# Two-layer decoder trunk: which FFN chunks go through the seven-product down projection

## The chip, the cores and the metric

The kernel runs on one core of a Trainium2 chip. The metric is the device time of one execution in microseconds, as the median of several executions; three of the kernel before gave 998.08, 990.7 and 993.01 us. The engines are TensorE (PE, with its weight loads shown apart as PEld), VectorE (DVE), ScalarE (ACT), GpSimd (POOL) and SyncE (SP), whose queue here issues the weight transfers.

## The reference

Two layers, each made of a half-step FFN, a token mixing and a second half-step FFN, on one sequence of 256 tokens with 1024 channels in float32. An FFN has 2816 hidden channels. What matters here is this:

```python
def swiglu(x, w_gate, w_up, w_down):
    return (jax.nn.silu(x @ w_gate) * (x @ w_up)) @ w_down
...
for l in range(DEPTH):
    x = layer_norm(ALPHA * x + 0.5 * swiglu(x, ffn1_gate[l], ...), ln1_g[l], ln1_b[l])
    proj = x @ w_in[l]            # short convolution, spatial gating, sparse attention
    ...
    mix = jnp.concatenate([y_a, y_b, y_c], axis=-1) @ w_out[l]
    x = layer_norm(ALPHA * x + mix, ln2_g[l], ln2_b[l])
    x = layer_norm(ALPHA * x + 0.5 * swiglu(x, ffn2_gate[l], ...), ln3_g[l], ln3_b[l])
```

## The kernel before

**Products.** Every large matrix product is done as three TensorE matmuls in a reduced float32 format: an operand is split into a high part (`hi`) and the rest (`lo`), and hi·hi, hi·lo and lo·hi are summed in PSUM. `mm3` (L248 to L250) does this for 512 output columns and `proj_chan` (L258 to L260) for the chunks whose output lies with channels on partitions, 256 tokens wide. `split_to` (L263) makes the two parts: ACT casts the high part, DVE subtracts it from the source.

**Weights.** All weights come in one order, made by `_plan()` (L72 on). `ensure` (L166 on) issues the next tile's transfer on SP into a `raw` buffer (5 of them), has ACT cast it (L190) and DVE subtract (L191), and puts the result into pools `hi` and `lo` (12 buffers each). It is called by `blocks` with a look-ahead of 7 tiles, so a tile's transfer and casts are written into the program some tiles ahead of its use.

**An FFN.** The hidden channels are cut into chunk 0 of 512 and chunks 1 to 9 of 256. Per chunk, `chan` or `tok` computes gate (`pg`) and up (`pu`), ACT makes `sg` = silu(pg) (L421), DVE makes `h` = pu·sg (L426), and h is split into `hTh` and `hTl` for the down projection. Chunk 0 is computed with tokens on partitions, so its h is transposed on PE (`trans`, L439) before it can be split. Each 128 rows of down weights are one tile `d` of 128x1024.

**Paired chunks.** In the FFNs for which `_paired` is 6 (three of the four; 0 for the first FFN of the program), the down projection of chunks 0 to 5 works on two `d` tiles at a time: the 2x2 blocks of tokens and output columns are multiplied with seven products `M1` to `M7` instead of eight (the Strassen and Winograd scheme). `pair_operands` prepares the weights' side: four DVE subtractions of 128x512 in the raw buffers (L202), one split of 512 columns (`b`), one of 1024, and, in `rest()`, two more splits of 1024 columns (the sums `th` and `sh`); `ensure` puts `rest()` off until a tile or so later. `left_sums` (L461 to L464) makes the left side's four sums `S` of 128x128, split by one more `split_to`. `combine` adds the seven results into x at the end.

**Banks.** While pairs run, `pg` and `pu` share one PSUM bank ("free"), the other holds M3, the "tr" pair holds M6 and M7, and the four "y" banks M1, M2, M4 and M5. So `pu` of a chunk can start only once ACT has read `pg` (`sg`), and the next `pg` only once DVE has read `pu` (`h`). Between the two stand the products of the chunk before: M1, M2, M4 and M5 (12 matmuls) between `pg` and `pu`, M6, M7 and M3 (9 matmuls) after `pu`.

**Order.** Each engine works through its own list, which a scheduler makes from the program, by priorities that the code raises at a few places (`tc.high_priority`). After the mixing, the output projection (`yo`) of tokens 0 to 127 is followed by the layer norm of that half (L374 to L380) and `to_xT` (L280), which transposes x and splits it into `xTh` and `xTl`, while PE does `yo` of the second half; the last attention heads' softmax (`P`, L833) and their transposes (`trp`, L837) fall into the same stretch.

## Time and profile before

| | before |
|---|---|
| median of three executions | 993.01 us (990.7 to 998.08) |
| profiled execution | 994.34 us |
| its span in the trace | 992.6 us |
| PE busy (matmuls) | 969.1 us (98%) |
| PE weight loads busy | 875.8 us (88%) |
| DVE busy | 734.8 us (74%) |
| ACT busy | 512.3 us (52%) |
| DMA | 55%, 183 GB/s over the span |
| granted TensorE clock | 0.999 of full speed |

The busy times are shares of the span. Matmuls are pipelined: a row's length is longer than the time from its start to the next one's start, so a run of matmuls is read by the distance between starts. A row's bracket gives the idle time of its engine ahead of it and what ended that.

### The profile page before, as it was taken

How to read it: one execution, taken by the hardware profiler on the slowest of the kernel's cores; microseconds unless marked ns; L12 is line 12 of the kernel's file. 1: busy time of each engine (PE TensorE's matmuls, PEld its weight loads, DVE VectorE, ACT ScalarE, POOL GpSimd, SP SyncE). 2: the span in 40 equal slices, each digit the busy share in tenths (PEclk: the TensorE clock that was granted, in tenths of full speed). 3: DMA queues.
4: the chain of work that ended last, by engine and by line, in shares of the span. 5: the costliest groups of instructions: out<-in, count | busy, mean ns of one | idle time of the engine just before them, and what ended most of it. 6: DMA issues, size and time to landing. Idle time of an engine off the chain costs nothing.

```text
span 992.6 us, 16879 instructions
## 1 busy us (share of the span) xinstructions
PE 969.1 (98%) x6765; PEld 875.8 (88%) x6765; DVE 734.8 (74%) x1094; ACT 512.3 (52%) x730; POOL 19.8 (2%) x42
## 2 busy tenths in 40 slices
PE   7999999999999999999999999999999999999996
PEld 5899999899878799999879899998988778989995
DVE  5755454586869978877598888848678797888844
ACT  6644444256556655555255556534475555556520
POOL 1000000010000000000000000000000000000000
PEclk9999999999999999999999999999999999999999
DMA  7977566284323557677245667764742245757611
GB/s 256 344 237 226 181 194 193 96 324 147 111 86 128 179 180 236 194 253 233 86 151 171 233 214 253 237 200 148 256 149 80 84 158 170 253 196 232 213 60 43
DMA packets 53069, 183.19 MB, mean 185 GB/s; under 512 B 6656, under 2 KB 7168, under 8 KB 52992
## 3 DMA queue, kind: packets, MB, share of 16 engines
q1 hardware_dynamic: 52992, 182.12, 55.0%
q8 instruction: 53, 0.87, 0.4%
q14 instruction: 24, 0.20, 0.1%
HBM read 181.05 MB, written 1.05 MB: 183 GB/s over the span
## 4 chain that ended last, share of the span: by engine, by line
PE 74%; DVE 11%; DMA 9%; issue 3%; ACT 3%; SPq 0%; DVEq 0%; ACTq 0%
DMA raw<-in_ws 8%; PE pu L258 6%; PE pu L260 6%; PE pu L259 6%; PE pg L258 5%; PE pg L260 5%; PE pg L259 5%; PE y L248 4%; PE y L250 4%; PE y L249 4%; DVE raw L202 3%; PE pc L258 3%; PE pc L260 3%; PE pc L259 3%; DVE lo L263 3%
## 5 line engine op out<-in xcount | busy, mean ns | idle before, releaser
L191 DVE TENSOR_TENSOR lo<-raw,hi 128x1024 fp32r<-128x1024 f32 (+3 forms) x284 | 336.6, 1200 | 115.2 <-ACT hi L190 113.5
L190 ACT CAST hi<-raw 128x1024 fp32r<-128x1024 f32 (+3 forms) x284 | 289.8, 1034 | 247.4 <-PE pu L259 64.7
L258 PE MATMUL pu<-xTh,hi 128*128 128x256 f32 x576 | 161.7, 281 | 3.4 <-ACT sg L421 3.4
L258 PE MATMUL pg<-xTh,hi 128*128 128x256 f32 x576 | 161.6, 281 | 0.5 <-DVE h L426 0.5
L260 PE MATMUL pu<-xTh,lo 128*128 128x256 f32 x576 | 160.9, 279 | 0.0
L260 PE MATMUL pg<-xTh,lo 128*128 128x256 f32 x576 | 160.8, 279 | 0.0
L259 PE MATMUL pu<-xTl,hi 128*128 128x256 f32 x576 | 160.8, 279 | 0.0
L259 PE MATMUL pg<-xTl,hi 128*128 128x256 f32 x576 | 160.8, 279 | 0.0
L258 PEld LDWEIGHTS pu<-xTh,hi 128*128 128x128 f32 x576 | 108.0, 188 | 7.1 <-ACT sg L421 5.9
L263 ACT CAST hi<-raw 128x1024 fp32r<-128x1024 f32 x63 | 66.2, 1052 | 90.5 <-DVE raw L202 46.5
L258 PEld LDWEIGHTS pg<-xTh,hi 128*128 128x128 f32 x576 | 108.1, 188 | 2.3 <-DVE h L426 1.2
L259 PEld LDWEIGHTS pu<-xTl,hi 128*128 128x128 f32 x576 | 107.9, 187 | 1.2
L260 PEld LDWEIGHTS pu<-xTh,lo 128*128 128x128 f32 x576 | 108.2, 188 | 0.2
L259 PEld LDWEIGHTS pg<-xTl,hi 128*128 128x128 f32 x576 | 107.9, 187 | 0.5
L260 PEld LDWEIGHTS pg<-xTh,lo 128*128 128x128 f32 x576 | 108.2, 188 | 0.0
L263 DVE TENSOR_TENSOR lo<-raw,hi 128x1024 fp32r<-128x1024 f32 x63 | 76.7, 1219 | 30.6 <-ACT hi L263 21.7
L258 PE MATMUL pc<-xTh,hi 128*128 128x256 f32 x256 | 73.0, 285 | 0.5 <-DVE kd L630 0.5
L248 PE MATMUL y<-hi,hTh 128*128 128x512 f32 x184 | 72.4, 394 | 0.0
L260 PE MATMUL pc<-xTh,lo 128*128 128x256 f32 x256 | 72.4, 283 | 0.0
L259 PE MATMUL pc<-xTl,hi 128*128 128x256 f32 x256 | 71.8, 281 | 0.0
L250 PE MATMUL y<-hi,hTl 128*128 128x512 f32 x184 | 71.8, 390 | 0.0
L249 PE MATMUL y<-lo,hTh 128*128 128x512 f32 x184 | 71.6, 389 | 0.0
(188 smaller groups left out, 1702.0 us busy)
## 6 DMA issues: line engine op xcount, KB each, us to landing
raw<-in_ws SPq DMA_DIRECT2D x312, 512.0 KB, 4.6
w<-in_ws SPq DMA_DIRECT2D x8, 512.0 KB, 6.2
lng<-in_ln SPq DMA_DIRECT2D x6, 512.0 KB, 6.8
lnb<-in_ln SPq DMA_DIRECT2D x6, 512.0 KB, 7.7
raw<-in_ws SPq DMA_DIRECT2D x8, 256.0 KB, 4.8
raw<-in_ws SPq DMA_DIRECT2D x4, 420.0 KB, 4.3
x<-in_x SPq DMA_DIRECT2D x4, 256.0 KB, 5.6
out<-x SPq DMA_DIRECT2D x4, 256.0 KB, 2.1
```

The costliest lines, as they stand in the source:

```text
L190: splits.append((ACT.copy(hi, raw), DVE.tensor_tensor(lo, raw, hi.bitcast(F32), ALU.subtract)))
L191: DVE.tensor_tensor(lo, raw, hi.bitcast(F32), ALU.subtract)))
L202: sub = lambda o, i, j: DVE.tensor_tensor(o, i, j, ALU.subtract)
L248: PE.matmul(o, lhsT=a[0], rhs=b[0], start=start, stop=False)
L249: PE.matmul(o, lhsT=a[0], rhs=b[1], start=False, stop=False)
L250: return PE.matmul(o, lhsT=a[1], rhs=b[0], start=False, stop=stop)
L258: PE.matmul(p[:, b, :], lhsT=hi, rhs=xTh[:, k, :], start=k == 0, stop=False)
L259: PE.matmul(p[:, b, :], lhsT=hi, rhs=xTl[:, k, :], start=False, stop=False)
L260: PE.matmul(p[:, b, :], lhsT=lo, rhs=xTh[:, k, :], start=False, stop=k == KC - 1)
L263: return ACT.copy(hi, src), DVE.tensor_tensor(lo, src, hi.bitcast(F32), ALU.subtract)
```

## The change

All four FFNs now have seven paired chunks, and these are chunks 1 to 7 in place of 0 to 5. Chunk 0's down weights are taken out of their place in the plan and put just ahead of chunk 9's; its down projection is done plainly at the end of the FFN, with chunks 8 and 9. With chunk 0 out of the pairs, no copy of its transposed h is needed (`hf` goes). The groups of products become M1, M2, M3, M5 and M6, M7, M4. `rest()` is put off one tile further. The raw pool grows from 5 to 7 buffers, `hi` and `lo` shrink from 12 to 11 each, and the work tag "a" grows from 9 to 12.

```diff
--- before.py
+++ after.py
@@ -32,9 +32,12 @@
 
 
 
+RAW, SPLIT = 7, 11
+
+
 def _paired(l, f):
 
-    return 0 if (l, f) == (0, 1) else 6
+    return 7
 
 
 def _w_in_groups():
@@ -83,7 +86,9 @@
                 for name in ("g", "u"):
                     step = _step(l, f, name, c)
                     out += [((l, f, name, c), k, step * fw, True) for k in range(0, KC, step)]
-                out += [((l, f, "d", c), k, 1024, True) for k in range(fw // 128)]
+
+                for c in ([0, c] if c == len(CHUNKS) - 1 else [c] if c else []) if _paired(l, f) else [c]:
+                    out += [((l, f, "d", c), k, 1024, True) for k in range(CHUNKS[c][1] // 128)]
     return out
 
 
@@ -137,9 +142,9 @@
     with ExitStack() as es:
         pool = lambda name, bufs, **k: es.enter_context(tc.tile_pool(name=name, bufs=bufs, **k))
         cst = pool("cst", 1)
-        rawp = pool("raw", 5)
-        hip = pool("hi", 12)
-        lop = pool("lo", 12)
+        rawp = pool("raw", RAW)
+        hip = pool("hi", SPLIT)
+        lop = pool("lo", SPLIT)
         wk = pool("wk", 9)
         sm = pool("sm", 3)
         lnp = pool("lnp", 1)
@@ -168,7 +173,7 @@
             while len(loaded) <= min(i, len(plan) - 1):
                 key, k, n, split, o = plan[len(loaded)]
                 src = A["ws"][o:o + 128 * n].rearrange("(p c) -> p c", p=128)
-                if len(key) == 4 and key[2] == "d" and key[3] < _paired(*key[:2]):
+                if len(key) == 4 and key[2] == "d" and 0 < key[3] <= _paired(*key[:2]):
                     raw = rawp.tile([128, n], F32, name="raw", tag="raw")
                     stream.append(SP.dma_start(raw, src))
                     if k % 2 == 0:
@@ -190,7 +195,7 @@
                 splits.append((ACT.copy(hi, raw),
                                DVE.tensor_tensor(lo, raw, hi.bitcast(F32), ALU.subtract)))
                 loaded.append((hi, lo))
-                while put_off and put_off[0][0] < len(loaded) - 1:
+                while put_off and put_off[0][0] < len(loaded) - 2:
                     put_off.pop(0)[1]()
 
         def pair_operands(ra, rb):
@@ -408,7 +413,7 @@
             def chan(name, c):
 
                 w = kslices((l, f, name, c), 256)
-                if c <= paired_chunks:
+                if 1 < c <= paired_chunks + 1:
                     p = ps.tile([128, 2, 256], F32, name="p" + name, tag=free, bufs=1)
                 else:
                     p = gu_bank([128, 2, 256], "p" + name)
@@ -429,8 +434,8 @@
             hT = {}
 
             def hpair():
-                return (wk.tile([128, 512], F32R, name="hTh", tag="a"),
-                        wk.tile([128, 512], F32R, name="hTl", tag="a"))
+                return (wk.tile([128, 512], F32R, name="hTh", tag="a", bufs=12),
+                        wk.tile([128, 512], F32R, name="hTl", tag="a", bufs=12))
 
             def trans(h, t):
                 tr = ps.tile([128, 512], F32, name="tr", tag="tr")
@@ -438,10 +443,6 @@
                     c = slice(i * 128, i * 128 + 128)
                     PE.transpose(tr[:, c], h[:, c], ident)
                 hT[0, t] = hpair()
-                if paired_chunks:
-                    hf[t] = wk.tile([128, 4, 128], F32, name="hf", tag="w")
-                    ACT.copy(hf[t].rearrange("p a b -> p (a b)"), tr)
-                    tr = hf[t].rearrange("p a b -> p (a b)")
                 split_to(*hT[0, t], tr)
 
             def stationary(c, t, i):
@@ -451,38 +452,31 @@
                 s = slice(i * 256 + t * 128, i * 256 + t * 128 + 128)
                 return hT[c][0][:, s], hT[c][1][:, s]
 
-            hf = {}
             left = {}
             M = {}
 
-            def left_sums(c, i, a11, a12, a21, a22):
-
+            def left_sums(c, h):
+
+                A = {(t, b): h[:, b * 256 + t * 128:b * 256 + t * 128 + 128] for t in range(2) for b in range(2)}
                 S = wk.tile([128, 4, 128], F32, name="S", tag="w")
-                DVE.tensor_tensor(S[:, 0, :], a21, a22, ALU.add)
-                DVE.tensor_tensor(S[:, 1, :], S[:, 0, :], a11, ALU.subtract)
-                DVE.tensor_tensor(S[:, 2, :], a11, a21, ALU.subtract)
-                DVE.tensor_tensor(S[:, 3, :], a12, S[:, 1, :], ALU.subtract)
+                DVE.tensor_tensor(S[:, 0, :], A[1, 0], A[1, 1], ALU.add)
+                DVE.tensor_tensor(S[:, 1, :], S[:, 0, :], A[0, 0], ALU.subtract)
+                DVE.tensor_tensor(S[:, 2, :], A[0, 0], A[1, 0], ALU.subtract)
+                DVE.tensor_tensor(S[:, 3, :], A[0, 1], S[:, 1, :], ALU.subtract)
                 hi, lo = hpair()
                 split_to(hi, lo, S.rearrange("p a b -> p (a b)"))
                 part = lambda j: (hi[:, j * 128:j * 128 + 128], lo[:, j * 128:j * 128 + 128])
-                left[c, i] = {5: part(0), 6: part(1), 7: part(2), 3: part(3)}
-
-            def left_side(c, i, m):
-                if m in (3, 5, 6, 7):
-                    return left[c, i][m]
-                t, b = {1: (0, 0), 2: (0, 1), 4: (1, 1)}[m]
-                return stationary(c, t, 2 * i + b)
+                left[c] = {5: part(0), 6: part(1), 7: part(2), 3: part(3),
+                           1: stationary(c, 0, 0), 2: stationary(c, 0, 1), 4: stationary(c, 1, 1)}
 
             def paired(c, ms):
 
+                w = blocks((l, f, "d", c))[0]
                 for m in ms:
                     if m not in M:
                         tag, bufs = {3: (held, 1), 6: ("tr", 2), 7: ("tr", 2)}.get(m, ("y", 4))
                         M[m] = ps.tile([128, 512], F32, name=f"M{m}", tag=tag, bufs=bufs)
-                    for i in range(CHUNKS[c][1] // 256):
-                        w = blocks((l, f, "d", c))[2 * i]
-                        mm3(M[m], left_side(c, i, m), w[m], c == 0 and i == 0,
-                            c == paired_chunks - 1 and i == CHUNKS[c][1] // 256 - 1)
+                    mm3(M[m], left[c][m], w[m], c == 1, c == paired_chunks)
 
             def combine():
 
@@ -535,22 +529,19 @@
                     if t == 1:
                         trans(h[0], 0)
                     h[t] = product(tok("u", t), sg)
-
-            if paired_chunks:
-                turns.append(1)
-                free, held = f"gu{len(turns) % 2}", f"gu{1 - len(turns) % 2}"
             for c in range(1, n):
+                in_pairs = 1 < c <= paired_chunks + 1
+                if in_pairs and c == 2:
+
+                    turns.append(1)
+                    free, held = f"gu{len(turns) % 2}", f"gu{1 - len(turns) % 2}"
                 p = chan("g", c)
                 with tc.high_priority(offset=60):
                     sg = gated(p)
                 if c == 1:
                     trans(h[1], 1)
-                if c <= paired_chunks:
-                    if c == 1:
-                        for i in range(2):
-                            a = lambda t, b: hf[t][:, 2 * i + b, :]
-                            left_sums(0, i, a(0, 0), a(0, 1), a(1, 0), a(1, 1))
-                    paired(c - 1, (1, 2, 4, 5))
+                if in_pairs:
+                    paired(c - 1, (1, 2, 3, 5))
                 elif not paired_chunks:
                     if c > 1 and c - 2 < n - late:
                         down([c - 2], 1)
@@ -559,14 +550,13 @@
                 pu = chan("u", c)
                 with tc.high_priority(offset=60):
                     hc = product(pu, sg)
-                if c <= paired_chunks:
-                    paired(c - 1, (6, 7, 3))
+                if in_pairs:
+                    paired(c - 1, (6, 7, 4))
                 hT[c] = hpair()
                 split_to(*hT[c], hc)
-                if c < paired_chunks:
-                    a = lambda t, b: hc[:, b * 256 + t * 128:b * 256 + t * 128 + 128]
-                    left_sums(c, 0, a(0, 0), a(0, 1), a(1, 0), a(1, 1))
-                if c == paired_chunks:
+                if c <= paired_chunks:
+                    left_sums(c, hc)
+                if paired_chunks and c == paired_chunks + 1:
                     combine()
                 if c == 2:
                     with tc.issue_after(stream[-1].ins):
@@ -575,9 +565,10 @@
                     with tc.issue_after(stream[-1].ins):
                         mid()
 
-            down(range(n - late, n - 1), 0)
+            cs = [*range(paired_chunks + 1, n - 1), 0] if paired_chunks else [*range(n - late, n - 1)]
+            down(cs, 0)
             down([n - 1], 0, end=True)
-            done = down(range(n - late, n), 1, end=True)
+            done = down([*cs, n - 1], 1, end=True)
             coef = 1.0 if paired_chunks else 2 * ALPHA
             layer_norm(0, y[0], coef, 4 * EPS, gb, last, [done[9], done[14]])
             layer_norm(1, y[1], coef, 4 * EPS, gb, last)
...
```

(The last three places give `kd`, `P` and `PT` the same `bufs=12`.)

What that moves shows at three places. The first is DVE at the start of the second FFN of layer 0, after the mixing, up to the first `h`. L202 is a subtraction of a pair's raw weights, L191 and L263 with `lo` are splits of plain and of pair weights. Before:

```order
L202 TENSOR_TENSOR raw<-raw 128x512
L263 TENSOR_TENSOR xTl<-tr,xTh 128x4x128 x2
L202 TENSOR_TENSOR raw<-raw 128x512
L263 TENSOR_TENSOR lo<-raw,hi 128x1024
L202 TENSOR_TENSOR raw<-raw 128x512 x2
L191 TENSOR_TENSOR lo<-raw,hi 128x1024
L202 TENSOR_TENSOR raw<-raw 128x512
L263 TENSOR_TENSOR lo<-raw,hi 128x1024
L202 TENSOR_TENSOR raw<-raw 128x512
L263 TENSOR_TENSOR lo<-raw,hi 128x1024
L202 TENSOR_TENSOR raw<-raw 128x512
L426 TENSOR_TENSOR h<-pu,sg 128x512
```

The same place after the change (L196 is the split of a plain tile, L431 is `h`):

```order
L384 SCALAR_TENSOR_TENSOR x_80<-x_80,mv,lng 128x512 x2
L385 SCALAR_TENSOR_TENSOR x_80<-x_80,rs,lnb 128x512 x2
L196 TENSOR_TENSOR lo<-raw,hi 128x1024
L268 TENSOR_TENSOR xTl<-tr,xTh 128x4x128 x2
L431 TENSOR_TENSOR h<-pu,sg 128x512
L196 TENSOR_TENSOR lo<-raw,hi 128x1024
L268 TENSOR_TENSOR b_3624<-raw,b_3624 128x512
L207 TENSOR_TENSOR raw<-raw 128x512 x2
```

The subtractions and splits of chunk 0's two pairs, which stood ahead of the first `h`, are gone from there; the first pair's work comes behind it.

The second place is ACT around `sg` in a paired chunk of that FFN. `hTh<-S` is the cast of the left sums; the two L263 (after: L268) casts of 128x1024 next to `sg` are those of a pair's `th` and `sh`. Before:

```order
L263 CAST hTh<-h 128x512
L190 CAST hi<-raw 128x1024 x2
L263 CAST hTh<-S 128x512
L263 CAST hi<-raw 128x1024
L421 ACTIVATE sg<-pg 128x512
L263 CAST hi<-raw 128x1024
```

After:

```order
L268 CAST hTh<-h 128x512
L195 CAST hi<-raw 128x1024
L268 CAST hTh<-S 128x512
L195 CAST hi<-raw 128x1024
L268 CAST hi<-raw 128x1024
L426 ACTIVATE sg<-pg 128x512
L268 CAST hi<-raw 128x1024
```

The cast of `th` still stands right ahead of `sg`, but a plain tile's cast now comes between it and the left sums.

The third place is DVE at the end of the mixing of layer 0, from the second half of the first layer norm on: x_79 is x of tokens 0 to 127, `P` the softmax of an attention head. Before:

```order
L374 SCALAR_TENSOR_TENSOR x_79<-x_79,yo 128x512
L831 RECIPROCAL su<-su 128x2
L375 BN_STATS st<-x_79 128x6
L833 TENSOR_SCALAR P<-P,su 128x256
L361 BN_AGGR mv<-st 128x2
L833 TENSOR_SCALAR P<-P,su 128x256
L363 TENSOR_SCALAR ve<-mv 128x1
L379 SCALAR_TENSOR_TENSOR x_79<-x_79,mv,lng 128x512 x2
L380 SCALAR_TENSOR_TENSOR x_79<-x_79,rs,lnb 128x512 x2
L191 TENSOR_TENSOR lo<-raw,hi 128x1024
L263 TENSOR_TENSOR xTl<-tr,xTh 128x4x128 x2
```

After:

```order
L196 TENSOR_TENSOR lo<-raw,hi 128x1024
L366 BN_AGGR mv<-st 128x2
L821 TENSOR_TENSOR su<-su,e_2994 128x2
L368 TENSOR_SCALAR ve<-mv 128x1
L384 SCALAR_TENSOR_TENSOR x_79<-x_79,mv,lng 128x512 x2
L385 SCALAR_TENSOR_TENSOR x_79<-x_79,rs,lnb 128x512 x2
L822 RECIPROCAL su<-su 128x2
L196 TENSOR_TENSOR lo<-raw,hi 128x1024
L824 TENSOR_SCALAR P<-P,su 128x256 x2
L196 TENSOR_TENSOR lo<-raw,hi 128x1024 x2
L268 TENSOR_TENSOR xTl<-tr,xTh 128x4x128
L196 TENSOR_TENSOR lo<-raw,hi 128x1024
```

The last head's `P` now comes behind the whole layer norm and a split, where it stood ahead of it; two more splits stand between it and `xTl`. On PE the transposes of this head (`trp`) now stand ahead of, and among, the transposes of x:

```order
L255 MATMUL yo<-hi,mixl 128x512
L828 MATMUL trp<-ident,P 128x128
L285 MATMUL tr<-ident,x_79 128x128 x4
L828 MATMUL trp<-ident,P 128x128 x3
L253 MATMUL pg<-hi,xTh 128x512
L254 MATMUL pg<-lo,xTh 128x512
L253 MATMUL pu<-hi,xTh 128x512
L285 MATMUL tr<-ident,x_79 128x128 x4
L849 MATMUL o<-PT,vv 64x128 x7
L255 MATMUL pg<-hi,xTl 128x512
```

Before, 34 `yo` matmuls stood between the transposes of x and the first `pg`, and no transpose of a head behind the layer norm; of these, after, most stand behind the first `pg`.

## Rows read from the trace of the kernel before

**Rows 1.** The page: busy time of each engine, and the chain of waits.

```profile
PE 969.1 (98%) x6765; PEld 875.8 (88%) x6765; DVE 734.8 (74%) x1094; ACT 512.3 (52%) x730; POOL 19.8 (2%) x42
...
PE 74%; DVE 11%; DMA 9%; issue 3%; ACT 3%; SPq 0%; DVEq 0%; ACTq 0%
```

**Rows 2.** The table of waits, PE: who was waited for, us in total, times, longest.

```profile
PE tr L439 <- DVE h L426: 4.5, 3, 1.8
PE pu L258 <- ACT sg L421: 3.4, 6, 1.2
...
PE pg L258 <- DVE h L426: 0.5, 1, 0.5
```

**Rows 3.** The page's groups: count, busy time, mean ns of one, then idle before.

```profile
L258 PEld LDWEIGHTS pg<-xTh,hi 128*128 128x128 f32 x576 | 108.1, 188 | 2.3 <-DVE h L426 1.2
...
L248 PE MATMUL y<-hi,hTh 128*128 128x512 f32 x184 | 72.4, 394 | 0.0
```

**Rows 4.** Timeline of PE, first and 27th matmul of one run: start, length, instruction.

```profile
175.26 0.40 PE L248 MATMUL y<-hi,hTh 128*128 128x512 f32 x1
...
181.19 0.39 PE L250 MATMUL y<-hi,hTl 128*128 128x512 f32 x1
```

**Rows 5.** Timeline of DVE ahead of the first h of FFN 2, layer 0.

```profile
319.75 0.68 DVE L202 TENSOR_TENSOR raw<-raw 128x512 f32<-128x512 f32 x1
...
329.17 1.22 DVE L263 TENSOR_TENSOR lo<-raw,hi 128x1024 fp32r<-128x1024 f32 x1
330.31 0.68 DVE L202 TENSOR_TENSOR raw<-raw 128x512 f32<-128x512 f32 x1
330.91 0.68 DVE L426 TENSOR_TENSOR h<-pu,sg 128x512 f32<-128x512 f32 x1
```

**Rows 6.** Timeline of PE at the same place.

```profile
331.74 0.63 PE L439 MATMUL tr<-ident,h 128*128 128x128 f32 x4 [1.77 <-DVE h L426]
```

**Rows 7.** Timeline of ACT around one sg that came late.

```profile
383.13 1.05 ACT L263 CAST hi<-raw 128x1024 fp32r<-128x1024 f32 x1 [2.05 <-DVE raw L202]
384.09 0.58 ACT L421 ACTIVATE sg<-pg 128x512 f32<-128x512 f32 x1
```

**Rows 8.** Timeline of PE at the same place: first M, last M, first pu.

```profile
381.29 0.40 PE L248 MATMUL M<-b,hTh 128*128 128x512 f32 x1
...
383.82 0.39 PE L250 MATMUL M<-hi,hTl 128*128 128x512 f32 x1
384.73 0.38 PE L258 MATMUL pu<-xTh,hi 128*128 128x256 f32 x1 [0.52 <-ACT sg L421]
```

**Rows 9.** Timeline of PE where M and pu alternate.

```profile
346.90 0.28 PE L260 MATMUL pu<-xTh,lo 128*128 128x256 f32 x1
347.11 0.50 PE L248 MATMUL M<-hi,hTh 128*128 128x512 f32 x1
```

**Rows 10.** Timeline of DVE at the end of the mixing, layer 0.

```profile
298.78 0.69 DVE L374 SCALAR_TENSOR_TENSOR x<-x,yo 128x512 f32<-128x512 f32 x1 [0.26 <-PE yo L250]
...
300.48 0.30 DVE L833 TENSOR_SCALAR P<-P,su 128x256 f32<-128x256 f32 x1
...
302.08 1.41 DVE L380 SCALAR_TENSOR_TENSOR x<-x,rs,lnb 128x512 f32<-128x512 f32 x2
303.41 1.22 DVE L191 TENSOR_TENSOR lo<-raw,hi 128x1024 fp32r<-128x1024 f32 x1
```

**Rows 11.** Timeline of PE at the same place.

```profile
303.49 1.04 PE L280 MATMUL tr<-ident,x 128*128 128x128 f32 x8
```

**Rows 12.** Windows: stretch, its length, busy time of each engine, clock, DMA share, GB/s.

```profile
25.00:50.00 25.00, 25.00 (x153) 22.16 (x152) 19.00 (x19) 14.92 (x16) 0.00 (x0) 1.00 0.95 347
```

**Rows 13.** Windows of the first FFN, and of one paired chunk of a later one.

```profile
50.00:100.00 50.00, 50.00 (x348) 46.62 (x347) 27.84 (x26) 24.16 (x26) 0.67 (x1) 1.00 0.71 230
...
408.69:424.84 16.15, 16.15 (x119) 15.25 (x117) 14.66 (x21) 10.65 (x13) 0.00 (x0) 1.00 0.62 192
```

**Rows 14.** Timeline of DVE in the chunk from 375.63 on: a wait for ACT.

```profile
378.07 1.23 DVE L263 TENSOR_TENSOR lo<-raw,hi 128x1024 fp32r<-128x1024 f32 x1 [1.68 <-ACT hi L263]
```

More of the change, by code (lines that the diff above doesn't have):

```diff
@@ L624, in mixing @@
             for i in range(2):
-                kd = wk.tile([128, 2, 16, 16], F32, name="kd", tag="a")
+                kd = wk.tile([128, 2, 16, 16], F32, name="kd", tag="a", bufs=12)
                 pe = sp["pe"][:, i, None, :]
@@ L822, in attend @@
                 DVE.tensor_reduce(nm[:, :m], sc, AX.X, ALU.max, negate=True)
-                P = wk.tile([128, m, w], F32, name="P", tag="a")
+                P = wk.tile([128, m, w], F32, name="P", tag="a", bufs=12)
                 su = sm.tile([128, 4], F32, name="su")
@@ L837, in attend @@
                     PE.transpose(tr[:, i, :], Pv[:, i * 128:i * 128 + 128], ident)
-                PT = wk.tile([128, 4, 128], F32, name="PT", tag="a")
+                PT = wk.tile([128, 4, 128], F32, name="PT", tag="a", bufs=12)
                 ACT.copy(PT, tr)
```

## The prediction

> **What bounds the kernel now.** The page's busy times and its chain of waits come first [rows 1]: PE is busy 98% of the span and carries 74% of the chain, so time goes only if PE has fewer matmuls or fewer gaps between them. The table of waits gives the gaps [rows 2]. Three times PE waits for the first `h` of an FFN (4.5 us), six times for `sg` (3.4) and once for `h` (0.5): 8.4 us, all in the three FFNs that pair. Then the timeline of PE tells what a matmul costs: in a run without a gap, 27 of them start within 181.19 − 175.26 = 5.93 us, or 0.228 us apart [rows 4], though a row lasts 0.39. DVE has 14.66 us of rows in a paired chunk of 16.15 [rows 13], which is the next bound.
>
> The sum is made against the profiled execution, 994.34 us (span 992.6). It lies 1.3 us above the median, inside a spread of 7.4 us between the three runs.
>
> **Fewer matmuls.** Before, chunk 0 gives two pairs and chunks 1 to 5 one each, 7 pairs in 3 FFNs; after, 7 in 4 FFNs. A pair saves one of eight products of three matmuls, so 7 × 3 = 21 matmuls of 512 columns fall away, all in the first FFN. At 0.228 us that is **−4.8 us**. By the row's mean length [rows 3] it would be 21 × 0.394 = 8.3, but rows overlap. The Trainium skill (Perfetto Trace Analysis, Identifying the Most-Contended Engine) calls matmul busy time a poor measure because matmuls are pipelined, and would have the weight loads looked at instead. By their row (188 ns, [rows 3]) the term would be −3.9 and PE would have 12% to spare; the distance between starts disagrees with that spare time, and I stay with it.
>
> **The first h of an FFN.** At the start of the FFN after the mixing, DVE works from 319.75 to 330.91 us on chunk 0's pairs and splits, and the first `h` is behind them [rows 5]; PE idles 1.77 us for it [rows 6]. The order now has a plain split and `xTl` ahead of `h`, and the pair's work behind it. So the three waits go: 4.5 us by rows, and 0.17 more each by the distance between starts (331.74 less the start before it is 2.17, of which 0.23 is the matmul): **−5.0 us**. Bounds: −5 if all go, 0 if the split ahead of `h` is as late as the pair work was.
>
> **The waits for the shared bank.** PE's 12 M matmuls (12 × 0.228 = 2.74 us) are all the cover that `sg` has. Where it came late, `th`'s cast had waited 2.05 us for a DVE subtraction and `sg` was queued behind it [rows 7], so `pu` started 0.91 us after the last M instead of 0.23 [rows 8]. Seven such places cost 3.9 us of idle time, or about 5.0 by starts. Now `rest()` is a tile later: a plain cast stands between, and the subtraction it needs has been issued longer ago. `sg` would end about 0.96 (the cast, 383.13 to 384.09) + 0.6 = 1.6 us after the last `pg` where nothing waits, a slack near 1 us. I take **−4.4 us**, leaving 0.6. Bounds: −5.0, and +3 if each of now 28 paired chunks waits as often as one of before's 18 (5.0 × 28/18 = 7.8). Putting the M3 product into the first group and M4 into the second changes no count; each group still has 12 and 9 matmuls.
>
> **Alternation.** With chunk 0's two pairs, M and `pu` matmuls alternate in chunk 1; a switch costs 0.21 us between starts in place of 0.12 [rows 9], and some 5 switches in each of 3 FFNs make 1.4. Chunk 1 now has no pair: **−1.5 us**.
>
> **End of the mixing.** Here the order gets worse, in both layers. Before, the last `P` is done at 300.48 and the layer norm's rows come after, until 303.41; PE transposes x at 303.49 and had 34 `yo` matmuls behind that [rows 10, 11]. After, one DVE list holds the second half's sum and statistics (0.6 + 0.6), a split (1.1), the norm (1.3 + 1.3, as 302.08 to 303.41), small operations (0.4), a further split (1.1) and two `P` (0.5): 7.0 us from the last `yo` of the first half, some 7.7 with ACT's part. PE's first transpose of this head is ahead of those of x, and behind 24 `yo` and an `o` (24 × 0.228 + 0.5 = 6.0): about 1.7 us of idle time. Then `pg` needs `xTh` (0.4 more) and `xTl`, behind two splits (2 × 1.14 + 0.6 after `P`), of which PE covers most with transposes and three matmuls: 0.5 more. Some 2.7 us, twice: **+5.5 us**. Bounds: 0 if ACT and the splits run ahead as they did, +8 if both splits' weights are late too.
>
> **The rest.** At the program's start x's second half is transposed between `pg` of the two halves, not within it, and ACT's `sg` and `xTh` cast and DVE's `xTl` come in between: +0.8 (0 to 2). More switches between matmul shapes: +0.5. Buffers: 7 raw and 11 split ones keep the look-ahead of 7 tiles; DMA stood at 347 GB/s in 25 to 50 us [rows 12], against 192 in a paired chunk [rows 13], so it costs nothing, covered by that lead; without the lead each tile of 512 KB would show its 1.5 us (512 KB at 347 GB/s). SP's queue holds the same tiles, four of them later. The added pairs in the first FFN put pair work on DVE: a pair takes 0.6 + 4 × 0.6 + 3 × 1.14 = 6.4 us where two plain splits take 2.3 (0.6 and 1.14 by the distance between starts, [rows 5]), and at most 5 × 0.6 = 3.0 of left sums, so 4.1 to 7.1 more for each chunk of 16 us; it is busy 27.84 of 50 there [rows 13], so this hides beside PE. `combine` (eleven operations of 0.6, 6.6 us on DVE) now lies beside chunk 9's `pg` and `pu`, 96 matmuls of 0.12 or 11.5 us.
>
> Sum: −4.8 − 5.0 − 4.4 − 1.5 + 5.5 + 0.8 + 0.5 = −8.9, so 985.4 for an execution like the profiled one and 984.1 against the median. I say **984.5 us**; its own range is 980 to 989.
>
> **Rivals.**
> *The end of the mixing costs nothing.* The last `P` would come early since its inputs are long there, and DVE idled for PE ahead of the norm before. Then 984.5 − 5.5 = 979. For it: that idle time (0.26 us, [rows 10]). Against it: each engine keeps to its list, and the list has `P` last. Chance 0.22.
>
> *The bank waits stay.* If `sg` is still late at before's rate per chunk, 7.8 − 0.6 = 7.2 are added: 991.7. For it: `th`'s cast still stands right ahead of `sg`. Against: 11 of the 18 paired chunks had no wait before. Chance 0.16.
>
> *The first FFN gains nothing.* It had no gaps before, and its weights arrive at 347 GB/s with DMA 95% busy up to 50 us [rows 12]. If the first pair's tiles come late, the 4.8 us are lost and about 1 more: 990. Chance 0.12.
>
> *DVE becomes the bound of a paired chunk: slower.* It has 14.66 us of rows in 16.15 [rows 13], and inside such a chunk it also waits for ACT, 1.68 us once [rows 14]. With 11 split buffers instead of 12 and sums cast later, casts come closer to their use. The point is where DVE's work and waits pass 16.15 us in a chunk; 1 us over in each of 28 chunks is +28, less the gains of waits already counted: about 1010. Against: rows overlap by 0.08 us, so 21 of them take some 13 us of issue. Chance 0.10.
>
> The forecast has the remaining 0.40. About 1% (983.1 and 1002.9) is what a measurement of this kernel can tell from no change. Faster by more than that: the first rival (0.21) and the lower part of the forecast (0.17), 0.38. Slower: the DVE rival, 0.09. Same: 0.53. The range from 976 to 994 holds the forecast and three rivals, with some of the first falling below it and the DVE case above.
>
> **What the profile after would show.** 21 fewer matmuls of 512 columns in `y` and M together; no `tr` wait for `h` at an FFN's start; at most two or three waits of `pu` for `sg`, of 0.2 to 0.3 us; a new wait of `trp` or `pg` at the end of each mixing, of 2 to 3 us, with `P` or `xTl` behind it on DVE; DVE's busy time higher by 30 to 50 us and still under PE's in every paired chunk. The forecast is wrong if waits for `sg` or `h` appear in most paired chunks, or if the end of the mixing shows no gap.

## The result, and the profile after

The changed kernel takes 982.04 us (median of 4 executions, 979.72 to 982.81) against 992.95: the ratio over all executions is 0.9879, 95% interval 0.9838 to 0.992 (the two medians alone give 0.9890). Run again beside the first experiments it took 982.28 against 992.2, ratio 0.9901 (0.9885 to 0.9917). So it is about 1.1% faster, 2.5 us below the forecast of 984.5 us and inside its own range of 980 to 989. One execution of the kernel `raw7_s12` below took 1350.53 us at a granted clock of 0.656, and its ratio leaves that one out.

The page after, busy times and chain of waits, to be held against [rows 1]:

```profile
PE 962.0 (98%) x6740; PEld 872.0 (89%) x6744; DVE 777.0 (79%) x1182; ACT 523.3 (54%) x746; POOL 30.3 (3%) x42
...
PE 95%; DVE 2%; ACT 1%; issue 1%; DMA 0%; SPq 0%; DVEq 0%; ACTq 0%
```

PE's share of the chain went from 74% to 95%: the work that ended last now runs almost without leaving PE. DVE is 42 us busier, and `M` and `y` have 972 matmuls in the trace where they had 993, 21 fewer. The whole table of waits of PE after, for [rows 2]:

```profile
PE tr L285 <- POOL blk L335: 3.5, 1, 3.5
PE pg L253 <- ACT xTh L268: 1.6, 3, 0.6
PE trp L828 <- DVE P L824: 1.4, 2, 0.7
PE tr L285 <- DMA x<-in_x: 1.1, 1, 1.1
PE scm L802 <- DVE QS L690: 0.4, 2, 0.2
```

The waits of `tr` for `h`, of `pu` for `sg` and of `pg` for `h` are gone from the list. New are two waits of `trp` for `P` and two of the three of `pg` for `xTh`, which lie at the ends of the two mixings; the third (0.29 us) is at the program's start. The row for `blk` is the program's first wait, which stood under the transfer of x before (3.64 us).

Cut at PE's first `pg` of the program, its first mixing matmul (`pt`), the first `pg` of layer 1 and the first `pt` of layer 1, the spans divide so (us):

| stage | before | after | after, again |
|---|---|---|---|
| up to the first pg | 8.19 | 6.44 | 7.46 |
| first FFN | 189.81 | 185.28 | 184.73 |
| mixing and second FFN, layer 0 | 300.46 | 298.38 | 299.41 |
| first FFN, layer 1 | 186.79 | 182.53 | 182.53 |
| mixing and second FFN, layer 1, end | 307.35 | 305.37 | 306.47 |
| span | 992.6 | 978.0 | 980.6 |

The two profiles after differ by 2.6 us, at the start and in the stages with a mixing. The first profile is of the fastest of its four executions, so the last column gives the change more nearly.

### The profile page after: what moved, and what is told of

Read it like the earlier page. It is cut to its first block, busy times and chain, and to the rows that moved or that the text cites. A ratio compares the mean times of both kernels' runs of the same rounds, so it can differ in the third digit from the quotient of the medians.

```text
span 978.0 us, 16978 instructions
## 1 busy us (share of the span) xinstructions
PE 962.0 (98%) x6740; PEld 872.0 (89%) x6744; DVE 777.0 (79%) x1182; ACT 523.3 (54%) x746; POOL 30.3 (3%) x42
## 4 chain that ended last, share of the span: by engine, by line
PE 95%; DVE 2%; ACT 1%; issue 1%; DMA 0%; SPq 0%; DVEq 0%; ACTq 0%
PE pu L263 7%; PE pg L263 7%; PE pg L265 7%; PE pu L265 7%; PE pg L264 7%; PE pu L264 7%; PE M L253 5%; PE M L255 5%; PE M L254 5%; PE pc L265 3%; PE pc L264 3%; PE pc L263 3%; PE y L253 3%; PE y L255 3%; PE y L254 3%; PE pg L253 2%
## 5 line engine op out<-in xcount | busy, mean ns | idle before, releaser
L195 ACT CAST hi<-raw 128x1024 fp32r<-128x1024 f32 (+2 forms) x270 | 273.6, 1033 | 234.9 <-PE pu L264 58.8
L196 DVE TENSOR_TENSOR lo<-raw,hi 128x1024 fp32r<-128x1024 f32 (+2 forms) x270 | 320.4, 1197 | 98.2 <-ACT hi L195 67.7
L263 PE MATMUL pu<-xTh,hi 128*128 128x256 f32 x576 | 161.7, 281 | 0.0
L263 PE MATMUL pg<-xTh,hi 128*128 128x256 f32 x576 | 161.3, 280 | 0.0
L268 ACT CAST hi<-raw 128x1024 fp32r<-128x1024 f32 x84 | 88.2, 1052 | 47.8 <-DVE raw L207 19.6
L263 PEld LDWEIGHTS pg<-xTh,hi 128*128 128x128 f32 x576 | 108.1, 188 | 1.3
L263 PEld LDWEIGHTS pu<-xTh,hi 128*128 128x128 f32 x576 | 108.1, 188 | 1.1
L268 DVE TENSOR_TENSOR lo<-raw,hi 128x1024 fp32r<-128x1024 f32 x84 | 101.3, 1220 | 2.0 <-ACT hi L268 1.5
L207 DVE TENSOR_TENSOR raw<-raw 128x512 f32<-128x512 f32 x112 | 76.8, 685 | 0.5
L263 PE MATMUL pc<-xTh,hi 128*128 128x256 f32 x256 | 72.4, 283 | 0.0
L253 PE MATMUL M<-hi,hTh 128*128 128x512 f32 x168 | 66.4, 395 | 0.0
L255 PE MATMUL M<-hi,hTl 128*128 128x512 f32 x168 | 65.8, 392 | 0.0
```

The costliest lines, as they stand in the source:

```text
L195: splits.append((ACT.copy(hi, raw), DVE.tensor_tensor(lo, raw, hi.bitcast(F32), ALU.subtract)))
L196: DVE.tensor_tensor(lo, raw, hi.bitcast(F32), ALU.subtract)))
L207: sub = lambda o, i, j: DVE.tensor_tensor(o, i, j, ALU.subtract)
L253: PE.matmul(o, lhsT=a[0], rhs=b[0], start=start, stop=False)
L255: return PE.matmul(o, lhsT=a[1], rhs=b[0], start=False, stop=stop)
L263: PE.matmul(p[:, b, :], lhsT=hi, rhs=xTh[:, k, :], start=k == 0, stop=False)
```

## Experiments

All ratios are to the kernel before, run on the same chip.

| kernel | median us | ratio (95%) |
|---|---|---|
| after_again | 982.28 | 0.9901 (0.9885 to 0.9917) |
| first_plain | 986.12 | 0.9939 (0.9925 to 0.9952) |
| rest_early | 981.95 | 0.9897 (0.9882 to 0.9911) |
| last_head | 980.37 | 0.9885 (0.987 to 0.9901) |
| raw5 | 989.04 | 0.9954 (0.9937 to 0.9971) |
| before_raw7 | 1008.46 | 1.0153 (1.0137 to 1.017) |
| rest_late_b | 991.68 | 0.999 (0.9975 to 1.0005) |
| six_all | 1001.82 | 1.0089 (1.0071 to 1.0108) |
| only_shift | 982.89 | 0.9898 (0.9882 to 0.9914) |
| raw7_s12 | 976.07 | 0.9827 (0.9811 to 0.9842) |
| pairs8 | 978.53 | 0.9854 (0.9839 to 0.987) |
| dve_two_more | 982.53 | 0.9891 (0.9875 to 0.9907) |

### The change again (after_again)

> The changed kernel once more, beside the others. Theory: 982 us within 2, no wait of pu or pg for sg or h in any FFN, no wait of tr for h. On the start: if the earlier start of the first pg (6.44 us after against 8.19 before) is the change's, it is again near 6.4; if it is how x's transfers happened to land, it lies anywhere from 6 to 8.5.

It came out so. The first `pg` started at 7.46 us, between the first profile's 6.44 and the 8.19 before; over all profiles here it lies between 6.44 and 8.55, whichever kernel, and follows the landing of x. No gain is claimed for the start.

### The first FFN's pairs undone (first_plain)

```diff
-    return 7
+    return 0 if (l, f) == (0, 1) else 7
```

> Only the first FFN's pairs undone (0 paired chunks there), the rest as after. Theory (21 matmuls at 0.228 us between starts, nothing else): 4.5 to 5 us more than after, about 986.7, all of it in the first FFN. Rival 1 (row length counts, 0.394 each): 8.3 more, 990. Rival 2 (the first FFN was bound by its start and gained nothing): within 1 us of after.

By medians 3.8 us more than after. Timelines of PE, the first `pg` and the first `pt`, first of the kernel without these pairs, then of after again:

```profile
7.59 0.78 PE L253 MATMUL pg<-hi,xTh 128*128 128x512 f32 x1
...
196.92 0.29 PE L253 MATMUL pt<-hi,xTh 128*128 128x280 f32 x1
```

```profile
7.46 0.78 PE L253 MATMUL pg<-hi,xTh 128*128 128x512 f32 x1
...
192.19 0.29 PE L253 MATMUL pt<-hi,xTh 128*128 128x280 f32 x1
```

The first FFN takes 189.33 us without pairs and 184.73 with: 4.6 us for 21 matmuls, 0.219 each. That is the distance between starts, not the row's length. By the length of weight loads the prediction had 3.9, which is nearer than the 8.3 by the length of matmuls. The Trainium skill (Perfetto Trace Analysis, Identifying the Most-Contended Engine) would have the busy share of weight loads looked at in place of that of matmuls to see how near the bound a kernel is. Here the 12% that weight loads left over were no spare time: they leave 11% now that PE hardly waits.

### The sums cast a block earlier again (rest_early)

```diff
-                while put_off and put_off[0][0] < len(loaded) - 2:
+                while put_off and put_off[0][0] < len(loaded) - 1:
```

> Only the point at which the sums th and sh are cast put back by one tile, the rest as after. Theory (the later cast took away the waits of pu for sg): waits of pu for sg return in a third or more of the 28 paired chunks, 5 to 8 us more than after, about 988. Rival (the waits went for another reason, such as chunk 0 leaving the pairs or two more raw buffers): within 1 us of after and no such waits.

The rival. No wait of PE for `sg` came back. ACT's waits show that the cast does wait more (the last row; there were 11 such waits of 19.6 us in the profile after), only not so long that `sg` behind it is late:

```profile
PE pg L253 <- ACT xTh L268: 1.6, 3, 0.6
PE trp L828 <- DVE P L824: 1.4, 2, 0.7
...
ACT hi L268 <- DVE raw L207: 52.3, 32, 2.4
```

One such place in the timeline of ACT, and then one of the kernel before at which PE waited 0.43 us for `sg`:

```profile
382.52 1.05 ACT L268 CAST hi<-raw 128x1024 fp32r<-128x1024 f32 x1 [2.40 <-DVE raw L207]
383.48 0.59 ACT L426 ACTIVATE sg<-pg 128x512 f32<-128x512 f32 x1
```

```profile
432.25 1.05 ACT L190 CAST hi<-raw 128x1024 fp32r<-128x1024 f32 x1 [1.60 <-DMA raw<-in_ws]
433.21 0.58 ACT L421 ACTIVATE sg<-pg 128x512 f32<-128x512 f32 x1
```

In the first, the cast of `th` waits longer than in [rows 7] (2.40 us against 2.05), yet `sg` starts 1.03 us after the chunk's first M (at 382.45), where it took 2.80 us in [rows 7, 8]. So the length of that wait doesn't tell whether `sg` is late. In the second, the cast ahead of `sg` is that of a plain tile and waits for its transfer; the same holds of the `sg` at 920.32 us. Two of the six waits before didn't stand behind `th`'s cast at all.

### The same edit on the kernel before (rest_late_b)

```diff
-                while put_off and put_off[0][0] < len(loaded) - 1:
+                while put_off and put_off[0][0] < len(loaded) - 2:
```

> The kernel before with the sums cast one tile later, nothing else. The prediction's step gives 4.4 us less than before, 987.8. The theory of the raw buffers gives no change, within 1.5 us of before, with waits of pu for sg as many as before.

The interval of the ratio holds 1, so the edit is worth 2.5 us at most and its sign isn't settled. PE's waits for `sg` fell from six to two, 3.4 to 2.1 us, and one for `h` grew to 0.9. These waits are of the slowest of twelve executions (996.89 us), so their sizes need not be those of the median. The prediction's step for this edit fails here: −4.4 us was not to be had from it.

### Five raw buffers again (raw5)

```diff
-RAW, SPLIT = 7, 11
+RAW, SPLIT = 5, 11
```

> After with 5 raw buffers in place of 7, nothing else. Casting the sums a block earlier brought no wait of pu for sg back, so the later cast is not what took these waits away. Theory now: the raw buffers did, since ACT's waits for weights to land went from 49.3 and 19.9 us before to 8.0 and 1.0 after. Then waits of pu for sg return, 4 to 8 us more than after, 986 to 990, and ACT waits for transfers again by 50 us or more. Rival (chunk 0 leaving the pairs took the waits away): within 1.5 us of after and no such waits.

The time is as the theory says, its place isn't, and ACT's waits for transfers come to 32 us, not 50. In the three later FFNs there is no wait for `sg` or `h`; all is lost in the first, which takes 198.76 − 8.47 = 190.29 us, no less than without pairs. There the weights are late. Timeline of ACT, then of PE, and the windows of PE behind it:

```profile
65.93 1.05 ACT L268 CAST hi<-raw 128x1024 fp32r<-128x1024 f32 x1 [4.12 <-DMA raw<-in_ws]
...
73.02 1.05 ACT L268 CAST hi<-raw 128x1024 fp32r<-128x1024 f32 x1 [1.63 <-DVE raw L207]
73.97 0.59 ACT L426 ACTIVATE sg<-pg 128x512 f32<-128x512 f32 x1
...
74.61 0.38 PE L263 MATMUL pu<-xTh,hi 128*128 128x256 f32 x1 [2.42 <-ACT sg L426]
```

```profile
72.00:76.00 4.00, 1.57 (x12) 1.39 (x12) 4.00 (x6) 1.54 (x2) 0.00 (x0) 0.97 0.56 146
76.00:80.00 4.00, 4.00 (x23) 4.00 (x23) 2.75 (x3) 2.00 (x2) 0.00 (x0) 0.60 0.90 292
```

A weight tile lands 4.12 us late for ACT; the pair's subtractions follow late on DVE, `th`'s cast waits for them, `sg` is behind the cast, and PE idles 2.42 us. In the window after, the granted clock is 0.60. So 7 raw buffers are worth some 5.5 us over 5, and that in the first FFN, which has pairs close to the program's start.

### More buffers on the kernel before (before_raw7)

```diff
-        rawp = pool("raw", 5)
-        hip = pool("hi", 12)
-        lop = pool("lo", 12)
+        rawp = pool("raw", 7)
+        hip = pool("hi", 11)
+        lop = pool("lo", 11)
```

> The kernel before with 7 raw and 11 split buffers, nothing else. Theory (raw buffers): the waits of pu for sg and of pg for h go, 4 to 5 us less than before, about 987.5, while the three waits of tr for h at the start of an FFN stay (4.5 us), since chunk 0's pairs are still ahead of h on DVE. Rival (chunk 0 leaving the pairs did both): within 1.5 us of before, waits as before.

Neither: 15 us slower. The waits of `pu` for `sg` went as the theory says. But three of `pg` for `sg` came (4.9 us), the three of `tr` for `h` grew from 4.5 to 6.7 us, and the ends of the mixings have the waits for `P` and `xTh` that the kernel after has (1.4 and 1.3 us). Timeline of PE, of DVE, and a window, at the start of layer 1's first FFN:

```profile
521.45 0.40 PE L250 MATMUL pg<-hi,xTl 128*128 128x512 f32 x1
523.52 0.39 PE L258 MATMUL pg<-xTh,hi 128*128 128x256 f32 x1 [1.68 <-ACT sg L421]
525.40 1.09 PE L439 MATMUL tr<-ident,h 128*128 128x128 f32 x4 [1.49 <-DVE h L426]
526.14 0.78 PE L248 MATMUL pu<-hi,xTh 128*128 128x512 f32 x1
...
528.42 0.63 PE L250 MATMUL pu<-hi,xTl 128*128 128x512 f32 x1
528.85 0.63 PE L248 MATMUL pu<-hi,xTh 128*128 128x512 f32 x1
...
523.44 1.22 DVE L191 TENSOR_TENSOR lo<-raw,hi 128x1024 fp32r<-128x1024 f32 x1
524.57 0.68 DVE L426 TENSOR_TENSOR h<-pu,sg 128x512 f32<-128x512 f32 x1
```

```profile
528.00:530.00 2.00, 2.00 (x6) 1.61 (x5) 0.49 (x1) 0.92 (x1) 0.00 (x0) 0.50 0.22 88
```

Between this FFN's first `pg` and its first `h`, DVE has the same pair work as in the kernel before (8 subtractions and 6 splits), but three plain splits in place of one, the last of them right ahead of `h`; `h` comes 20.56 us after that `pg`, where it came 18.22 us after it. PE stands still for most of 521.7 to 525.4, and then the granted clock is at its lower level until some 531 us: matmuls that are 0.228 us apart [rows 4] are 0.43 apart there. Each of the three pairing FFNs is 6.7 to 6.8 us longer than in after again.

The start of the FFNs isn't all of it. Against the kernel before, layer 1's first FFN is 2.5 us longer (189.32 us), and the two stages of a mixing and a second FFN are 5.4 and 5.3 us longer. If the second FFNs lose 2.5 us as well, the mixings lose some 5.6 us together, an estimate, about what raw7_s12 below gives back by one more split buffer. This exchange of split buffers for raw ones does harm without the shift; which part of it the raw ones have was not run.

### Six paired chunks in the first FFN too, on the kernel before (six_all)

```diff
-    return 0 if (l, f) == (0, 1) else 6
+    return 6
```

> The kernel before with 6 paired chunks in the first FFN too, nothing else. Theory: 21 matmuls fall away there, 4.6 us, and the first FFN takes on the waits of the other three (1.5 of tr for h, about 1.5 of pu for sg, 0.5 of alternation), so 0 to 2 us less than before, about 991. Rival (pairs of chunk 0 cost nothing where weights come late anyway): 4.6 less, 987.6.

Worse than either: 8.4 us slower by medians. The waits of PE:

```profile
PE pu L258 <- ACT sg L421: 9.3, 8, 1.7
PE tr L439 <- DVE h L426: 8.0, 4, 3.9
```

and their longest, with the window behind it:

```profile
36.98 0.66 PE L439 MATMUL tr<-ident,h 128*128 128x128 f32 x4 [3.86 <-DVE h L426]
```

```profile
38.00:42.00 4.00, 4.00 (x23) 4.00 (x23) 4.00 (x4) 4.00 (x6) 0.00 (x0) 0.57 0.79 249
```

The pairs of chunk 0 hold back the first `h` by 3.86 us at the program's start, and the clock falls behind it. The 4.6 us of the 21 matmuls are lost, and 8.4 us more. By the profile the first FFN is 5.6 us longer than before (195.42 us), and layer 1's first, which the edit leaves alone, 2.0: its waits at the shared bank came to 3.5 us where they were 1.9.

### Only the shift (only_shift)

```diff
-RAW, SPLIT = 7, 11
+RAW, SPLIT = 5, 12
...
-    return 7
+    return 0 if (l, f) == (0, 1) else 7
-                while put_off and put_off[0][0] < len(loaded) - 2:
+                while put_off and put_off[0][0] < len(loaded) - 1:
-                    paired(c - 1, (1, 2, 3, 5))
+                    paired(c - 1, (1, 2, 4, 5))
-                    paired(c - 1, (6, 7, 4))
+                    paired(c - 1, (6, 7, 3))
```

> Of the change only the shift of the pairs from chunks 0 to 5 to chunks 1 to 7, in the three FFNs that paired before: the first FFN plain, 5 raw and 12 split buffers, sums cast as early as before, the groups of products as before. Theory (chunk 0's two pairs ahead of the first h put DVE behind, and the late weights, casts and sg of the later chunks follow from that): no wait of tr for h and at most one of pu for sg, 9 to 11.5 us less than before, about 983, and since the end of the mixing keeps its order, no gap there. Rival (the shift takes only the waits of tr for h and the alternation; 5 raw buffers, the early cast or the old groups bring the waits for sg back): 6.5 less than before, about 987.

The theory: 9.9 us less than before, as much as the whole change. The waits of PE and the waits of ACT for the pair's subtractions and for weights, against ACT's three waits before of 46.5 us (21 times, longest 5.1), 49.3 and 19.9:

```profile
PE tr L285 <- DMA x<-in_x: 5.7, 2, 3.6
PE pu L263 <- ACT sg L426: 1.7, 1, 1.7
...
ACT hi L268 <- DVE raw L207: 44.1, 25, 2.4
ACT hi L195 <- DMA raw<-in_ws: 34.4, 51, 2.5
...
ACT hi L268 <- DMA raw<-in_ws: 2.6, 1, 2.6
```

Of the seven waits at the shared bank one is left, and no wait of `tr` for `h`. The `sg` of the one that is left starts 7 us behind a cast that waited 2.62 us for its transfer (579.73 us). ACT's casts wait for subtractions and transfers about as often as before, but never over 2.6 us. At 5 raw buffers, with the early cast and the old groups, the shift does it. (The work tag "a" keeps the 12 buffers of the kernel after here; with 8, in raw7_s12 below, there is no wait at the shared bank either.) That the waits go with the shift is shown; how chunk 0's two pairs made casts late several chunks on isn't.

### The last head ahead of the layer norm (last_head)

```diff
-                    attend(t, slots, sc.pop(i))
+                    if i >= len(steps) - 1:
+                        with tc.high_priority(offset=300):
+                            attend(t, slots, sc.pop(i))
+                    else:
+                        attend(t, slots, sc.pop(i))
```

> After, with the last attention head of each layer raised in priority, so that its P comes ahead of the layer norm on DVE and PE keeps yo between the transposes of x and the first pg. Theory (the new gaps at the end of the mixing, 0.72 and 0.64 us idle and their restarts, 1.7 us in each layer, come from that order): both gaps go, 3.4 us less than after, about 978.6. Rival (the gap moves to pg's wait for xTl, or the layer norm comes late instead): within 1 us of after.

In between: 1.9 us less by medians. First the place in the kernel after, PE and then DVE, for [rows 10, 11]:

```profile
297.53 0.39 PE L255 MATMUL yo<-hi,mixl 128*128 128x512 f32 x1
298.64 0.30 PE L828 MATMUL trp<-ident,P 128*128 128x128 f32 x1 [0.72 <-DVE P L824]
298.78 0.60 PE L285 MATMUL tr<-ident,x 128*128 128x128 f32 x4
299.22 0.49 PE L828 MATMUL trp<-ident,P 128*128 128x128 f32 x3
300.34 0.50 PE L253 MATMUL pg<-hi,xTh 128*128 128x512 f32 x1 [0.64 <-ACT xTh L268]
...
295.51 1.41 DVE L385 SCALAR_TENSOR_TENSOR x<-x,rs,lnb 128x512 f32<-128x512 f32 x2
...
297.00 1.23 DVE L196 TENSOR_TENSOR lo<-raw,hi 128x1024 fp32r<-128x1024 f32 x1
298.15 0.61 DVE L824 TENSOR_SCALAR P<-P,su 128x256 f32<-128x256 f32 x2
```

PE waits for `P` (the softmax), which DVE has behind the layer norm and a split, then for `xTh`, the chain that the prediction drew. With the last head raised both waits are gone from the table, and a shorter one, of `pg` for `xTl`, came in:

```profile
PE pg L255 <- DVE xTl L268: 0.3, 2, 0.2
PE pg L253 <- ACT xTh L268: 0.3, 1, 0.3
```

### Twelve split buffers (raw7_s12)

```diff
-RAW, SPLIT = 7, 11
+RAW, SPLIT = 7, 12
```

(All five tiles of the work tag "a" also get `bufs=8` in place of 12, to make room.)

> After with 12 split buffers in place of 11, the room taken from the work tag (8 in place of 12), 7 raw buffers kept. With 12 the scheduler keeps the order before at the end of the mixing. Theory (that gap is the order's, and 8 work buffers are enough): no wait there, 3 us less than after, about 979. Rival (8 work buffers make casts of h wait for a free one): as slow as after or slower, with new waits of M for hTh.

Better than the theory: 976.07 us, 6.2 less than after, and the fastest kernel of this study. Its waits of PE, all of them:

```profile
PE tr L285 <- POOL blk L335: 3.6, 1, 3.6
PE tr L285 <- DMA x<-in_x: 1.9, 1, 1.9
PE pg L253 <- ACT xTh L268: 0.3, 1, 0.3
```

Against after again the first FFNs are equal within 0.5 us (185.17 and 184.73 us, 182.53 and 182.53), and the two stages with a mixing are 2.86 and 3.36 us shorter. In the first of these, by PE's starts, `trp` and `yo` give 1.5 of the 2.86 (6.07 to 5.13 and 24.66 to 24.08), which are the gaps; most of the rest is spread over `pc`, `pg`, `pt` and `scm`, whose order differs too.

The edit changes two pools, but the other runs tell which one it was. The waits of `trp` for `P` and of `pg` for `xTh` at the end of the mixings are in the profile of every kernel with 11 split buffers except last_head, with 9 or 12 work buffers and 5 or 7 raw ones, and in none with 12 split buffers, with 8, 9 or 12 work buffers. Why the scheduler's order depends on that pool isn't shown.

### Eight paired chunks (pairs8)

```diff
-    return 7
+    return 8
-            layer_norm(0, y[0], coef, 4 * EPS, gb, last, [done[9], done[14]])
+            layer_norm(0, y[0], coef, 4 * EPS, gb, last, [done[6], done[10]])
```

> After with eight paired chunks (1 to 8), the layer norm's start moved to later products of the shorter end. 12 more matmuls fall away, 2.7 us. Theory (combine's eleven DVE operations, 6.6 us, were hidden by chunk 9's gate and up products, which are now gone from behind them): the end of each FFN waits 3 to 6 us for combine, so 10 to 20 us more than after, about 995. Rival (the downs of the remaining chunks can start in another bank, or combine's parts free their banks one by one): 2.7 less than after, 979.5.

The rival: 3.75 us less than after again, of which 12 matmuls are 2.7; the rest lies within the intervals. Timeline of PE at the end of the first FFN, the last M and the first `y`, and DVE beside it:

```profile
173.99 0.39 PE L255 MATMUL M<-hi,hTl 128*128 128x512 f32 x1
174.22 0.39 PE L253 MATMUL y<-hi,hTh 128*128 128x512 f32 x1
...
168.76 0.69 DVE L483 TENSOR_TENSOR x<-x,M 128x512 f32<-128x512 f32 x1
```

`y` follows M without a gap. `combine` had read its first products before the last M ended, so banks can have come free, and its other operations run beside `y`. The cover that the prediction named wasn't needed.

### Two more subtractions per pair on DVE (dve_two_more)

```diff
             def rest():
                 th, tl = both(ra)
                 sh, sl = both(rb)
+                DVE.tensor_tensor(tl, ra, th.bitcast(F32), ALU.subtract)
+                DVE.tensor_tensor(sl, rb, sh.bitcast(F32), ALU.subtract)
```

> After with two more 128x1024 subtractions on DVE for each pair (each repeats the one that made a sum's low part, with the same result): 28 times 2.28 us of work without use. By rows DVE has 13.7 us in 16.0 of a paired chunk, so with 2.44 more it stands at the chunk's length. If DVE keeps what the rows leave over: within 3 us of after. If waits for ACT inside the chunk count with its work, as in the prediction's slower rival: each of 28 chunks is longer by 0.5 to 1 us, 14 to 28 more, 996 to 1010, with waits of pg for h and pu for sg in most paired chunks.

No change (0.25 us by medians). One window of 16 us within paired chunks, first after and then with the added work:

```profile
387.00:403.00 16.00, 16.00 (x118) 15.11 (x117) 13.69 (x19) 8.46 (x10) 0.00 (x0) 1.00 0.65 201
```

```profile
387.00:403.00 16.00, 16.00 (x118) 15.11 (x117) 15.99 (x22) 9.30 (x11) 0.00 (x0) 1.00 0.57 184
```

DVE can be busy 15.99 of 16.00 us and PE still doesn't wait; its table of waits has none in a paired chunk. That the look-ahead is what allows it isn't shown.

## Why the prediction was right, and where it wasn't

**Fewer matmuls (−4.8): right**, 4.6 by the first FFN's length, with a condition that its sum left out: it needs the raw buffers. With 5 of them the first FFN takes 190.29 us and the third rival (the first FFN gains nothing) would have come true.

**The first h (−5.0): right.** The three waits went, and with only the shift too. The size of this term by itself was not measured.

**The shared bank (−4.4): the size right, the reason wrong.** The step that failed is "Now `rest()` is a tile later": undone, nothing comes back; done alone on the kernel before, the waits are two in place of six and the time is the same within its interval. What took the waits away is the shift: with none of the other edits to casts, groups and buffers, it left one of seven. I had read the row of [rows 7] as a matter of where one cast stands; but casts that wait as long there do no harm after the shift, and two of the six `sg` waits stood behind a transfer. That −4.4 came out all the same is luck. Which of the other edits took the last wait (1.72 us) isn't settled.

**Alternation (−1.5; its own working gives 1.4): fits, as a remainder.** With only the shift the stage of layer 0's mixing and second FFN is 3.65 us shorter; the wait for `h` is 1.94 of it, the two for `sg` 0.68 + 0.60, and 0.43 are left, or 1.3 for three FFNs if each has as much.

**End of the mixing (+5.5): the mechanism right, its parts off.** The gaps are 0.72 and 0.64 us of idle time in each layer where I had 1.7, 0.4 and 0.5: `P` came 7.2 us after the last `yo` of the first half (291.43 to 298.67, 7.0 to 7.7 said), but PE had 6.3 us of other work, not 6.0, and there was no wait for `xTl`: it was done at 301.62 us, before the 14 matmuls of `o` began at 301.68 and the first matmul that reads it at 302.69. Yet against the kernel with 12 split buffers the two stages lose 2.9 and 3.4 us, 6.2 in all, since rows elsewhere in the mixing are dearer too. The gaps that the prediction named are 2.7 us of idle time in both layers; that the whole comes near +5.5 is in part luck.

**Buffers (0): wrong both ways.** "It costs nothing" was said of 7 raw and 11 split buffers. The raw ones are worth some 5.5 us in the first FFN, which I had booked under its matmuls; the split ones set off the order at the end of the mixing, which I had put to the change's order in general.

**The start (+0.8) and switches (+0.5):** the new wait is 0.29 us; the landing of x varies by more.

The forecast came out 2.5 us too high. By the runs the sum would read −4.6 (the first FFN) − 9.9 (the shift) − 1.9 (the last wait at the bank, by starts) + 6.2 (the split buffers) = −10.2 us, where −8.9 was forecast and −9.9 to −10.9 measured. The rivals: the end of the mixing did cost; the bank waits did not stay; DVE did not become the bound, and had room for two more operations per pair.

## What to carry to other kernels

A wait far into a stage can go with work that is put ahead of the stage's first result: try that work elsewhere before adding buffers, since with 7 raw and 11 split buffers alone two more splits came ahead of that result, and it was later. Test each edit of a bundle on its own, both added to the old kernel and taken from the new: here the shift of the pairs alone is worth as much as the whole change, the pairs in the first FFN give 4.6 us but only with more raw buffers, the later cast does nothing that was measured, and one split buffer less gives 6 us away. When a pool's size changes, compare the order of instructions far from that pool; with 12 split buffers and 8 work buffers the kernel takes 976.07 us. Eight pairs on top of that was not run.

## What the runs showed of the hardware that was not expected

The granted clock of TensorE fell to its lower level (0.50, 1.2 of 2.4 GHz) after PE had stood still for most of 3.7 us in one kernel (before_raw7), and stayed there for some 6.8 us, from 524.3 to 531.2. It was 0.57 and 0.60 on average over 4 us after waits of 3.86 and 2.42 us in two others (six_all, raw5), and at 1.00 after that. A stop cost up to 2.4 us more than its idle time: 24 `pu` matmuls from 526.14 on took that much longer than at 0.228 us each. The length of a wait alone doesn't tell: after a single wait of 1.77 us [rows 6] the granted clock stays at 1.00, while in the profile of rest_late_b it is at 0.50 from 389 to 391 us after a single wait of 1.75 us, and at 1.00 again from 392.
